# Sliding-window queries computed between the steps of the latent attention, four modulation vectors made by TensorE

## The chip, the cores and the metric

The kernel runs on one core of one Trainium2 chip. The metric is the device time of one execution in microseconds (us). A core has five engines that each take their instructions in order: PE (TensorE, matrix products; its weight loads are listed as PEld), DVE (VectorE), ACT (ScalarE), POOL (GpSimd) and SP (SyncE, which here only issues DMAs; ACT and SP have DMA queues of their own).

## The reference, cut to what matters

The network has 512 tokens of width 1024 and four layers; the change is in the first, the even block: latent attention (MLA, 8 heads) beside sliding-window attention with sinks (SWA, 8 heads, 2 key heads, window 128).

```python
z = h @ w_in
z_cq, z_ckv, z_kr, z_sq, z_sk, z_sv, z_gate = split_cols(z, EVEN_SPLITS)
q  = (rmsnorm(z_cq, q_norm) @ w_uq)      # latent queries, 8 x 96
kv = (rmsnorm(z_ckv, kv_norm) @ w_ukv)   # latent keys and values, 8 x 128
...
o_mla = mla_attention(q_nope, q_rope, k_nope, k_rope, v_mla)
q_s = apply_rope(z_sq, cos_h, sin_h)     # 8 x 64
k_s = apply_rope(z_sk, cos_h, sin_h)     # 2 x 64
o_swa = swa_sink_attention(q_s, k_s, v_s, sinks)
o = jnp.concatenate([o_mla, o_swa], axis=-1) * jax.nn.silu(z_gate)
return o @ w_out
```

Each layer is modulated by vectors of the condition alone: `mod = cond @ ada_w[i] + ada_b[i]` gives scale, shift and gate, each a 1024 x 1024 matrix times a vector. They don't depend on the tokens and are made while other work runs.

## The kernel before

Products of float32 numbers are made as three products of split parts (high x high, high x low, low x high), in the helper `mm3` (L208), so most PE rows of the profile carry L208. Weights are loaded by SP as `raw`, cast by ACT (L222) and their low part made by DVE or POOL (L225). A product of a block of 128 tokens with 512 columns and depth 1024 is 8 x 3 = 24 matmuls of 128x512.

The even block goes through these steps: the input products cq and ckv; SQ (`ev_sq`, 4 blocks of tokens, 96 matmuls of 128x512, rotation on DVE, result written to the DRAM tensor `sq_e`); the latent up-products uq and ukv, written to the DRAM tensor `qk_e` (L852) and read back by heads (L863), where `heads_T` (L650) transposes them in the PSUM tag "tq", which has one bank. `mla()` then runs 16 steps (4 pairs of heads x 4 blocks of queries): scores, softmax (DVE L633 mask and minimum, ACT L635 exponential, DVE L636, POOL L640), transposes of the probabilities (`p_T` L663, L665), and products with the values (L682). `swa()` runs 16 steps of the same kind with at most 256 keys. Both are generators. `weave` runs one step of the attention, and then as many units of a second generator, `fill`, as its share allows; a unit is three matmuls of 512 columns. Before, `fill` holds 72 units: gates 1, 2 and 3 (8 units each), sk (16) and the gates 4, 6, 5, 7. 52 of them go beneath `mla()`. Gate 0 is run ahead. `issue_after` and a scheduler that works from a modelled timeline set the final order of each engine's instructions, so units move somewhat from where the code has them.

The modulation vectors are made by `ada`, piece by piece: each piece (`tick`) loads half a megabyte of the matrix (`araw`, L495, two buffers) and does one step. In the even block four vectors are made, each in 2 halves x 4 steps, 32 steps. Before, the step is `step`: two DVE operations on 128x512 (L540 for the first, else L542), and at the end of a half a group of four small products with ones (L548) and one addition (L550). The other form, `step_pe`, used elsewhere in this program (in the conv stage, L522), lets PE multiply: eight matmuls of 32 columns by 128 in a PSUM bank, then one DVE addition of 128x128 (L524); a step's products are issued one step after its load (`ADA_LAG`).

Of the kernel before, what the change touches and what calls it, by code (L numbers as in the profile page):

```python
# [20 lines left out]
KC = D // P  # L21
# [18 lines left out]
STRICT = 0  # L40
FD = 6
ADA_OFF = 0
W_MLA = 52
ONDVE = (0, 1, 2)
W_FOX = 3
MAIN_OFF = 0
# [13 lines left out]
TV = 0  # L60
TVE = 3
# [3 lines left out]
SQF = 0  # L65
G0 = 2
# [46 lines left out]
class K:  # L113
# [647 lines left out]
    def even(self, act, gs):  # L761
        nc, h = self.nc, self.h
        w = h["ev_w_in"][0]
# [41 lines left out]
            nc.scalar.dma_start(out=sqd[tb * P:(tb + 1) * P, 8:10, :], in_=t.rearrange("p (n d) -> p n d", d=64))  # L805
            nc.scalar.copy(out=SV[:, tb], in_=ps[:, 128:256])

        if TV == 1:
            self.tick_every = TVE
        o = self.otile()  # L810
        if SQF:
            self.run(self.gates(act, w, 1440, o, (0, 1)[:G0]))
        else:
            self.gemm_x(act, w, 672, 512, KC, ev_sq)
        if TV == 2:
            self.tick_every = TVE
        cT = [self.b4() for _ in range(5)]
        for c in range(5):
            ps = self.psum("tp")
# [39 lines left out]
        def mla():  # L859
            self.npool = NPL[0]  # L860
            def load(hd):
                t = self.tmp()[:, :768].rearrange("p (tb d) -> p tb d", d=192)
                nc.scalar.dma_start(out=t, in_=qk[:, hd, :].rearrange("(tb p) d -> p tb d", p=P))  # L863
                return (self.heads_T(t, 96, lambda s, tb: s[:, tb, 0:96], msc),
                        self.heads_T(t, 96, lambda s, tb: s[:, tb, 96:192]))
            nxt = [load(0), load(1)]
            for c in range(4):
                qk2 = nxt
                pv = self.psum("pv")
                for qb in range(NTB):  # L870
                    n = (qb + 1) * P
                    ps = []
                    for qT, kT in qk2:
                        sc = self.scores(slice(0, 96), qT, kT, qb, 0, n)
                        ps.append(self.softmax(sc, n, self.cst[:, C_CM + 512 - n:C_CM + 512]))
                    self.pv_pair(pv, [[V[b][:, h_ * 64:h_ * 64 + 64] for b in range(qb + 1)] for h_ in (2 * c, 2 * c + 1)], ps, qb)
                    if qb in (1, 2) and c < 3:
                        nxt = (nxt if qb == 2 else []) + [load(2 * c + 1 + qb)]
                    yield
                self.tick(TM)  # L880
                self.pv_out(o[:, c, :], pv)

        def swa():
            self.npool = NPL[1]
            t = self.tmp()[:, :512].rearrange("p (tb d) -> p tb d", d=P)
            nc.scalar.dma_start(out=t, in_=sqd[:, 8:10, :].rearrange("(tb p) n d -> p tb (n d)", p=P))
            kT = self.heads_T(t, 128, lambda s, tb: s[:, tb])

            def load(i):
                t = self.tmp()[:, :512].rearrange("p (tb r d) -> p tb r d", r=2, d=64)  # L890
                for r in range(2):
                    nc.scalar.dma_start(out=t[:, :, r, :], in_=sqd[:, i + 4 * r, :].rearrange("(tb p) d -> p tb d", p=P))
                return self.heads_T(t, 128, lambda s, tb: s[:, tb].rearrange("p r d -> p (r d)"), -0.125)

            qTs = {0: load(0), 1: load(1)}
            for hd in (0, 4, 2, 6):
                r = hd // 4
                pv = self.psum("pv")
                for qb in range(NTB):
                    k0 = max(0, qb - 1)  # L900
                    nb = qb - k0 + 1
                    n = nb * P
                    ps = []
                    for h_ in (hd, hd + 1):
                        sc = self.scores(slice(64 * r, 64 * r + 64), qTs[h_ % 4], kT, qb, k0 * P, n)
                        ps.append(self.softmax(sc, n, self.cst[:, C_SM + 256 - n:C_SM + 256], sink=self.nsink[:, h_:h_ + 1]))
                    self.pv_pair(pv, [[SV[:, b, r * 64:r * 64 + 64] for b in range(k0, qb + 1)]] * 2, ps, qb)
                    if hd == 4 and qb < 2:
                        qTs[qb + 2] = load(qb + 2)
                    yield  # L910
                self.tick(TSW)
                self.pv_out(o[:, 4 + hd // 2, :], pv)

        def fill():
            if SQF:
                yield from self.gates(act, w, 1440, o, (0, 1)[G0:])
                yield from self.gemm_xs(act, w, 1184, 256, KC, ev_sk)
                yield from self.gates(act, w, 1440, o, (2,))
                yield from self.gemm_xs(act, w, 672, 512, KC, ev_sq)
                yield from self.gates(act, w, 1440, o, (3, 4, 6, 5, 7))  # L920
                return
            yield from self.gates(act, w, 1440, o, (1, 2, 3))
            yield from self.gemm_xs(act, w, 1184, 256, KC, ev_sk)
            yield from self.gates(act, w, 1440, o, (4, 6, 5, 7))

        self.lo_pool = LOP[0]
        if not SQF:
            self.run(self.gates(act, w, 1440, o, (0,)))
        g = fill()
        self.weave(mla(), 16, g, W_MLA + 16 * SQF)  # L930
        self.weave(swa(), 16, g, (96 - 8 * G0 if SQF else 76) - W_MLA)
        return o


# [706 lines left out]
def build(tc, h, upto=99):  # L1641
    nc = tc.nc
    with ExitStack() as es:
        k = K(tc, h, es)
# [9 lines left out]
        with k.scope(t4=5, xn=1, SB=2, wide=8, wsb=2, rep=1, prow=1, col=1):  # L1654
            cc, cc2, act, gs = k.start(x_in, h["c"], h["c_2"], wa[0], ba[0], h["g_pre"][0], h["ev_w_in"][0], 384)
# [5 lines left out]
        def first(i, mixer, act, xsrc, xdst, wout, **bufs):  # L1661
            with tc.tile_pool(name="xp", bufs=1, reuse_waits="tile") as k.xp:
                with k.scope(**bufs):
                    k.tick_every = TO if i else 1000
                    k.ada_pool = AP[i]
                    rows = [k.ada(cc, wa[i], ba[i], 2048, "gatepost", h["g_post"][i])]
                    if i == 0:
                        rows += [k.ada(cc, wa[1], ba[1], 1024, "scale", h["g_pre"][1]),
                                 k.ada(cc, wa[1], ba[1], 0, "shift")]
                    else:  # L1670
                        rows += [k.ada(cc2, wa2[0], ba2[0], 1024, "scale", h["norm1_g_2"][0]),
                                 k.ada(cc2, wa2[0], ba2[0], 0, "shift")]
                        mods[0] = [k.ada(cc2, wa2[0], ba2[0], 2048, "gate")]
                    if G2 == 2 + i:
                        mods["g2"] = k.ada(cc2, wa2[0], ba2[0], 5120, "gate")
                    o = mixer(act)
                    k.flush()
                    k.lo_pool, k.tick_every = 0, 1
                    k.ada_pool = ()
                    if MK & 4:  # L1680
                        k.mark()
                with k.scope(t4=3, rows=3, oT=2, hl2=3):
                    GG, S, B = [k.spread(r) for r in rows]
                    o = k.out_first(o, wout, xsrc, xdst, GG, S, B)
                    if MK & 8:
                        k.mark()
                    return o

        act = first(0, lambda a: k.even(a, gs), act, x_in, out if upto == 1 else x1, h["ev_w_out"][0], t4=4, ru=1, s=6, pt=6, b4=6, V=4, SV=1)
        if upto == 1:  # L1690
            return
        act = first(1, k.odd, act, x1, out if upto == 2 else x2, h["od_w_out"][0], t4=2, ru=1, hn=1, s=6, pt=6, b4=4, Vd=4, V=4, foxA=1, foxB=1, foxBh=2, lp=1)
        if upto == 2:
            return
# [61 lines left out]
        with tc.tile_pool(name="xp", bufs=1, reuse_waits="tile") as k.xp:  # L1756
            act, xr = second(0, act, k.conv, x2, t4=4, u=3, dw=1, dwr=1, w4=1, u4=4, dg=3)
# [27 lines left out]
        with tc.tile_pool(name="xp", bufs=1, reuse_waits="tile") as k.xp:  # L1785
            act, xr = second(1, act, k.hgrn, x4, V=8, X=3, F=1, op=2, hn=1, gt=1, AT=1, Ad=2, T0=1, T1=1, T2=1, T3=1, T4=1, T5=1, T6=1)
# [41 lines left out]
```

## Time and profile before

| | us |
|---|---|
| median of 3 runs (lowest, highest) | 2098.3 (2095.98, 2098.57) |
| the profiled execution | 2094.94 |
| its span from first to last instruction | 2093.2 |
| PE busy | 1956.3 |
| DVE busy | 1345.0 |
| ACT busy | 861.8 |
| POOL busy | 733.1 |

The span is that of the profiled execution, and all rows below are of it. Busy time is the union of an engine's instructions; PE matmuls overlap each other in the records, so what a matmul costs in a dense stretch is read from the distance of two starts. PEclk is the granted clock of TensorE, 1.00 at 2.4 GHz and 0.50 at 1.2 GHz.

### The profile page before, as it was taken

Reading aid. Unit: us, or ns where it says so; the run is one execution under the profiler, and the core shown is the slowest. Engines: PE = TensorE matmul, PEld = TensorE weight load, DVE = VectorE, ACT = ScalarE, POOL = GpSimd, SP = SyncE. Lnnn points to the kernel's source line nnn. Section 1 sums busy time; section 2 is a strip of 40 time slices with the busy share of each in tenths; the row PEclk is TensorE's granted clock in tenths of the full one; section 3 lists DMA queues with packets and bytes.
Section 4 is the critical chain, followed back from the end, with each engine's and each line's share of the span. In section 5 each row is a group of like instructions: output and inputs, shape, how many; then the busy total and the mean of one; then the engine's idle time right before and its main releaser. Section 6 shows DMA issues by size and latency. Waiting matters only on the chain.

```text
span 2093.2 us, 32588 instructions
## 1 busy us (share of the span) xinstructions
PE 1956.3 (93%) x12759; PEld 1585.6 (76%) x12759; DVE 1345.0 (64%) x1979; ACT 861.8 (41%) x1461; POOL 733.1 (35%) x660
## 2 busy tenths in 40 slices
PE   7799999798999999879899999999999998999998
PEld 5688668565667787458788989877877778898896
DVE  5356775535545479547987748667786858485673
ACT  4345553133554432143434435343554534353452
POOL 1233334221233333015232331456675544223232
PEclk9999979997999999899999999999999999999999
DMA  8484655277343436832554225453322322242331
GB/s 311 129 230 136 180 166 161 80 164 145 80 97 104 149 117 187 223 99 71 178 178 153 87 75 182 134 152 103 103 83 82 121 83 80 91 131 71 121 102 60
DMA packets 225745, 272.09 MB, mean 130 GB/s; under 512 B 26682, under 2 KB 145689, under 8 KB 225592
## 3 DMA queue, kind: packets, MB, share of 16 engines
q1 hardware_dynamic: 188982, 232.83, 37.8%
q10 hardware_dynamic: 36610, 37.18, 5.9%
q8 instruction: 101, 1.65, 0.3%
q14 instruction: 52, 0.43, 0.1%
HBM read 253.57 MB, written 16.40 MB: 129 GB/s over the span
## 4 chain that ended last, share of the span: by engine, by line
PE 41%; DVE 12%; issue 4%; DMA 4%; POOL 2%; ACT 1%; ACTq 0%; SPq 0%; POOLq 0%; DVEq 0%
PE mm L208 23%; PE mm L1223 4%; PE sc L208 4%; PE sc L1223 3%; PE tp L1223 3%; DVE acc L542 2%; DVE ol L1343 2%; DVE hl L201 1%; DMA ud<-u 1%; DVE hl L225 1%; DMA raw<-in_ada_w_dram 1%; PE pv L208 1%; DVE X L1585 1%; DMA u<-ud 1%; DMA raw<-in_mlp_w_dram 0%
## 5 line engine op out<-in xcount | busy, mean ns | idle before, releaser
L208 PE MATMUL mm<-hTh,hl 128*128 128x512 f32 (+2 forms) x1200 | 375.3, 389 | 3.0 <-DVE V L201 1.5
L222 ACT CAST hl<-raw 128x1024 fp32r<-128x1024 f32 (+2 forms) x219 | 224.4, 1033 | 245.7 <-PE mm L208 142.8
L208 PE MATMUL mm<-hl,hid 128*128 128x512 f32 x1344 | 316.9, 395 | 4.9 <-DVE hid L201 3.3
L225 DVE TENSOR_TENSOR hl<-raw,hl 128x1024 fp32r<-128x1024 f32 (+2 forms) x190 | 251.0, 1331 | 78.3 <-ACT hl L222 77.8
L208 PEld LDWEIGHTS mm<-hl,hid 128*128 128x128 f32 x1344 | 251.9, 188 | 64.7 <-DVE hid L201 4.3
L208 PEld LDWEIGHTS mm<-hTh,hl 128*128 128x128 f32 (+1 forms) x1200 | 221.6, 191 | 51.6 <-issue 3.8
L208 PE MATMUL mm<-hl,hTh 128*128 128x512 f32 (+3 forms) x752 | 223.6, 375 | 26.5 <-DVE t L621 11.0
L208 PE MATMUL mm<-hTl,hl 128*128 128x512 f32 (+2 forms) x600 | 232.8, 388 | 0.1
L1140 POOL TENSOR_TENSOR xr<-xr,t 128x512 f32<-128x512 f32 x56 | 80.3, 1433 | 305.6 <-DVE t L1137 304.2
L208 PEld LDWEIGHTS mm<-hl,hTh 128*128 128x128 f32 x752 | 141.8, 199 | 52.2 <-ACT t L788 8.7
L542 DVE SCALAR_TENSOR_TENSOR acc<-araw,ccol,acc 128x512 f32<-128x512 f32 x154 | 135.0, 876 | 36.3 <-DMA araw<-in_ada_w_dram 24.3
L640 POOL TENSOR_TENSOR s<-s,sm 128x256 f32<-128x256 f32 (+3 forms) x112 | 82.8, 740 | 193.1 <-DVE sm L636 184.9
L200 ACT CAST hl<-raw 128x1024 fp32r<-128x1024 f32 x84 | 86.8, 1048 | 135.9 <-PE mm L208 111.3
L208 PE MATMUL mm<-hl,hTl 128*128 128x512 f32 (+3 forms) x376 | 139.8, 372 | 0.4 <-DVE hTl L458 0.4
L201 DVE TENSOR_TENSOR hl<-raw,hl 128x1024 fp32r<-128x1024 f32 x84 | 131.3, 1578 | 13.6 <-ACT hl L200 12.9
L208 PEld LDWEIGHTS mm<-hTl,hl 128*128 128x128 f32 (+1 forms) x600 | 114.5, 191 | 23.6 <-issue 2.0
L1203 POOL TENSOR_TENSOR raw<-raw,raw 128x1024 f32<-128x1024 f32 x28 | 76.2, 2722 | 144.4 <-DVE rows L1203 95.1
L225 POOL TENSOR_TENSOR hl<-raw,hl 128x1024 fp32r<-128x1024 f32 x29 | 73.1, 2520 | 120.5 <-ACT hl L222 120.5
L635 ACT ACTIVATE s<-s,sm 128x256 f32<-128x256 f32 (+5 forms) x128 | 69.6, 544 | 95.0 <-DVE sm L633 89.4
L1137 DVE TENSOR_TENSOR t<-mm,rows 128x512 f32<-128x512 f32 x56 | 38.5, 687 | 106.8 <-PE mm L208 103.1
L208 PE MATMUL sc<-b,b 64*128 64x256 f32 (+7 forms) x384 | 94.5, 361 | 10.5 <-DVE sm L633 8.2
L1588 POOL TENSOR_TENSOR X<-X,T 128x512 f32<-128x512 f32 x56 | 74.2, 1330 | 50.5 <-ACT op L1548 32.7
(366 smaller groups left out, 3960.4 us busy)
## 6 DMA issues: line engine op xcount, KB each, us to landing
raw<-in_mlp_w_dram SPq DMA_DIRECT2D x128, 512.0 KB
araw<-in_ada_w_dram SPq DMA_DIRECT2D x72, 512.0 KB
raw<-in_hgrn_w_in_dram SPq DMA_DIRECT2D x40, 512.0 KB
araw<-in_w_ada_dram SPq DMA_DIRECT2D x32, 512.0 KB
raw<-in_od_w_in_dram SPq DMA_DIRECT2D x32, 512.0 KB
raw<-in_ada_w_dram SPq DMA_DIRECT2D x24, 512.0 KB
rows<-row SPq DMA_DIRECT2D x16, 512.0 KB
raw<-in_conv_w_in_dram SPq DMA_DIRECT2D x16, 512.0 KB
```

The source lines that it names most:

```text
L200: nc.scalar.copy(out=hi, in_=src)
L201: nc.vector.tensor_tensor(out=lo, in0=src, in1=hi.bitcast(F32), op=ALU.subtract)
L208: self.nc.tensor.matmul(out, lhsT=lt[a], rhs=rt[b], start=start and n == 0, stop=stop and n == 2)
L222: self.nc.scalar.copy(out=hi, in_=raw[:, :n])
L225: eng.tensor_tensor(out=lo, in0=raw[:, :n], in1=hi.bitcast(F32), op=ALU.subtract)
L542: eng.scalar_tensor_tensor(out=acc, in0=raw[:, k], scalar=c, in1=acc, op0=ALU.mult, op1=ALU.add)
L635: nc.scalar.activation(out=s[:, :m], in_=s[:, :m], func=AF.Exp, scale=-1.0, bias=mn, accum_out=sm)
L640: nc.gpsimd.tensor_tensor(out=p, in0=p, in1=r.to_broadcast([P, n]), op=ALU.mult)
L1140: eng.tensor_tensor(out=xs, in0=xs, in1=t, op=ALU.add)
L1203: eng.tensor_tensor(out=out, in0=x, in1=y, op=f)
L1223: nc.tensor.matmul(ps[:, m * 256:m * 256 + 256], lhsT=ws[n][:, a, k, m * P:m * P + P], rhs=parts[n][b][:, k], start=m + k + t == 0, stop=m ...
L1588: nc.gpsimd.tensor_tensor(out=xk, in0=xk, in1=cap(Tt, 1, [(row - 1, 2), (2, nb), (0, hh)]), op=ALU.mult)
```

## The change

SQ and gate 0 are no longer run ahead of the attention but are part of `fill`, which now holds 112 units in the order gate 0, sk, gates 1 and 2, SQ, gates 3, 4, 6, 5, 7; 80 go beneath `mla()`. Branches of the old code that were not in use (`SQF`, `TV`) are deleted. In the even block the four vectors are made by `step_pe`, with its products in the PSUM tag "tq", the bank that `heads_T` uses.

```diff
@@ module
-W_MLA = 52
+W_MLA = 80
@@ even(), ahead of the attention
         o = self.otile()
-        if SQF:
-            self.run(self.gates(act, w, 1440, o, (0, 1)[:G0]))
-        else:
-            self.gemm_x(act, w, 672, 512, KC, ev_sq)
...
         def fill():
...
-            yield from self.gates(act, w, 1440, o, (1, 2, 3))
+
+            yield from self.gates(act, w, 1440, o, (0,))
             yield from self.gemm_xs(act, w, 1184, 256, KC, ev_sk)
-            yield from self.gates(act, w, 1440, o, (4, 6, 5, 7))
+            yield from self.gates(act, w, 1440, o, (1, 2))
+            yield from self.gemm_xs(act, w, 672, 512, KC, ev_sq)
+            yield from self.gates(act, w, 1440, o, (3, 4, 6, 5, 7))
 
         self.lo_pool = LOP[0]
-        if not SQF:
-            self.run(self.gates(act, w, 1440, o, (0,)))
         g = fill()
-        self.weave(mla(), 16, g, W_MLA + 16 * SQF)
-        self.weave(swa(), 16, g, (96 - 8 * G0 if SQF else 76) - W_MLA)
+        self.weave(mla(), 16, g, W_MLA)
+        self.weave(swa(), 16, g, 112 - W_MLA)
@@ first()
                     k.ada_pool = AP[i]
+                    k.ada_pe, k.ada_ps = i == 0, "tq"
...
                     k.ada_pool = ()
+                    k.ada_pe = False
```

On PE, just ahead of the first score of the latent attention (`sc`, the row of 128x128), the order before has the gate products (`mm` from `hTh`, `hTl`) around the transposes of the first two heads (L650), and a vector's closing group (L548):

```order
405 L548 MATMUL mm_1513<-acc_1208,ones 32x128 x4
406 L208 MATMUL mm_1441<-hTl,hl_1438 128x512
407 L208 MATMUL mm_1441<-hTh,hl_1438 128x512
408 L650 MATMUL tq_1223<-cst,t_212_1213 96x128 x4
409 L208 MATMUL mm_1583<-hTh,hl_1580 128x512
410 L208 MATMUL mm_1583<-hTl,hl_1580 128x512
```

At the same place the changed kernel has sk's products (128x256), and the two transposes stand back to back:

```order
326 L208 MATMUL mm_1309<-hl_1202,hTl 128x256
327 L208 MATMUL mm_1309<-hl_1202,hTh 128x256
328 L650 MATMUL tq_1034<-cst,t_187_1032 96x128 x4
329 L650 MATMUL tq_1042<-cst,t_187_1032 96x128 x4
330 L208 MATMUL sc_1069<-b_191_1047,b_189_1039 128x128
331 L208 MATMUL mm_1399<-hl_1197,hTh 128x256
```

The first score is row 418 of PE before and row 330 afterwards: SQ, the gates 1 and 2 and a part of 3 have moved behind it, and two of sk's four blocks in front of it.

On PE in the last pair of heads of the latent attention (scores `sc`, transposes `tp`, value products `pv`) the order before has gate products as filler between the attention's own:

```order
660 L663 MATMUL tp_2008<-cst,s_1994 128x128 x3
661 L208 MATMUL sc_2161<-b_422_1945,b_420_1937 128x128 x3
662 L682 MATMUL pv_1823<-pt_2006,V_939 64x128
663 L208 MATMUL mm_2333<-hTh,hl_2330 128x512 x2
664 L208 MATMUL mm_2333<-hTl,hl_2330 128x512
665 L208 MATMUL mm_2333<-hTh,hl_2330 128x512 x2
666 L208 MATMUL mm_2333<-hTl,hl_2330 128x512
```

The changed kernel has steps of the vectors there (L522, in the bank `tq`), and no gate products:

```order
677 L650 MATMUL tq_2053<-cst,t_444_2043 96x128 x4
678 L208 MATMUL sc_2203<-b_448_2058,b_446_2050 128x128
679 L208 MATMUL sc_2259<-b_424_1964,b_422_1956 128x256 x3
680 L522 MATMUL tq_2135<-araw_1982,ccol_93 32x128 x8
681 L208 MATMUL sc_2203<-b_448_2058,b_446_2050 128x128 x2
682 L522 MATMUL tq_2167<-araw_2133,ccol_93 32x128 x8
683 L208 MATMUL sc_2271<-b_448_2058,b_446_2050 128x256 x3
684 L208 MATMUL sc_2312<-b_424_1964,b_422_1956 128x384 x3
685 L663 MATMUL tp_2219<-cst,s_2207 128x128
686 L522 MATMUL tq_2179<-araw_2165,ccol_93 32x128 x8
```

Ten such steps stand in rows 680 to 734; the gate products pause from row 674 to 738 and then reach to row 875, where before the last of them stood some 70 rows ahead of the end of SWA.

On DVE in SWA (row L633 is a softmax's first operation) the order before has an accumulation between almost every two softmaxes:

```order
298 L633 ISA s_2467,sm_2468<-sc_2463,cst,nsink 128x128
299 L633 ISA sm_2468 128x1
300 L542 SCALAR_TENSOR_TENSOR acc_2856<-araw_2865,ccol_93,acc_2856 128x512
301 L636 RECIPROCAL sm_2470<-sm_2469 128x1
302 L633 ISA s_2496,sm_2497<-sc_2492,cst,nsink 128x256
303 L633 ISA sm_2497 128x1
304 L542 SCALAR_TENSOR_TENSOR acc_2856<-araw_2865,ccol_93,acc_2856 128x512
```

The changed kernel has one addition for about two softmaxes:

```order
269 L633 ISA s_2587,sm_2588<-sc_2583,cst,nsink 128x256
270 L633 ISA sm_2588 128x1
271 L524 TENSOR_TENSOR arow_2366<-tq_2727,arow_2366 128x128
272 L636 RECIPROCAL sm_2590<-sm_2589 128x1
273 L633 ISA s_2600,sm_2601<-sc_2596,cst,nsink 128x256
274 L633 ISA sm_2601 128x1
```

The accumulations of 128x512 (L542) are gone from DVE's queue in this stretch, and additions of 128x128 (L524) stand in their place.

## Rows read from the trace of the kernel before

**Rows 1.** page: busy time of each engine, and shares of the chain that ended last:
```profile
PE 1956.3 (93%) x12759; PEld 1585.6 (76%) x12759; DVE 1345.0 (64%) x1979; ACT 861.8 (41%) x1461; POOL 733.1 (35%) x660
...
PE 41%; DVE 12%; issue 4%; DMA 4%; POOL 2%; ACT 1%; ACTq 0%; SPq 0%; POOLq 0%; DVEq 0%
```
**Rows 2.** windows: stages of the even block; columns engines, PEclk, DMA, GB/s:
```profile
80.30:151.40 71.10, 71.10 (x349) 60.26 (x348) 32.79 (x54) 28.12 (x53) 20.55 (x21) 1.00 0.70 186
151.40:168.00 16.60, 14.09 (x72) 11.72 (x72) 10.86 (x28) 7.58 (x21) 5.66 (x7) 0.79 0.62 197
168.00:238.30 70.30, 70.30 (x504) 55.66 (x503) 51.93 (x139) 38.53 (x100) 21.65 (x31) 1.00 0.56 162
238.30:275.00 36.70, 35.04 (x220) 23.92 (x223) 26.31 (x81) 19.04 (x61) 17.85 (x40) 1.00 0.45 130
275.00:308.10 33.10, 31.34 (x147) 19.65 (x147) 22.71 (x65) 15.21 (x50) 12.62 (x26) 0.59 0.56 164
```
**Rows 3.** windows: the start of the latent attention and the tail of SWA:
```profile
151.40:156.60 5.20, 2.69 (x19) 1.94 (x18) 4.67 (x8) 1.93 (x5) 2.38 (x2) 1.00 0.72 216
...
156.60:163.40 6.80, 6.80 (x31) 6.16 (x30) 4.89 (x17) 3.70 (x11) 2.21 (x4) 0.50 0.92 304
...
279.50:306.80 27.30, 27.30 (x116) 17.04 (x116) 17.58 (x53) 11.29 (x39) 10.64 (x21) 0.50 0.58 164
```
**Rows 4.** timeline, PE: dense gate products; first score at 151.44 (start, us, instruction):
```profile
151.21 0.39 PE L208 MATMUL mm<-hTh,hl 128*128 128x512 f32 x1
151.44 0.23 PE L208 MATMUL sc<-b,b 96*128 96x128 f32 x1
```
**Rows 5.** timeline, PE, conv stage: steps of L522 between products:
```profile
821.33 0.63 PE L208 MATMUL mm<-hTh,hl 128*128 128x512 f32 x2
...
821.89 0.64 PE L522 MATMUL tp<-araw,ccol 128*32 128x128 f32 x16
...
822.46 0.50 PE L208 MATMUL mm<-hTl,hl 128*128 128x512 f32 x1
```
**Rows 6.** timeline, PE, SWA: one L548 group and what follows:
```profile
258.75 0.43 PE L548 MATMUL mm<-acc,ones 128*32 128x128 f32 x8
...
259.11 0.43 PE L682 MATMUL pv<-pt,SV 128*64 128x128 f32 x2
...
259.47 0.61 PE L208 MATMUL sc<-b,b 64*128 64x256 f32 x3
```
**Rows 7.** timeline: sinks DMA and the ckv stop:
```profile
58.74 0.28 SPq L779 DMA_DIRECT2D sm<-in_ev_sinks_dram  x1
...
75.15 0.29 PEld L208 LDWEIGHTS mm<-hl,hTh 128*128 128x128 f32 x1 [8.72 <-ACT t L788]
```
**Rows 8.** timeline: qk written, read back and transposed:
```profile
131.69 0.52 ACTq L852 DMA_DIRECT2D qk_e<-t  x1
...
136.49 0.39 ACTq L863 DMA_DIRECT2D t<-qk_e  x1
...
145.14 0.60 PE L650 MATMUL tq<-cst,t 128*96 128x128 f32 x4
```
**Rows 9.** groups of instructions by form, 145 to 308.2: the vector accumulation:
```profile
L542 DVE SCALAR_TENSOR_TENSOR acc<-araw,ccol,acc 128x512 f32<-128x512 f32 x56 | 47.4, 847 | 1.6 <-DMA araw<-in_ada_w_dram 1.4
```
**Rows 10.** windows of L542 alone: DVE busy (count), PEclk, DMA, GB/s:
```profile
238.30:275.00 36.70, 12.15 (x14) 1.00 0.45 130
```
**Rows 11.** timeline, tail of SWA: a softmax behind an accumulation:
```profile
278.87 0.61 PE L208 MATMUL sc<-b,b 64*128 64x256 f32 x3 [0.88 <-DVE sm L633]
...
279.33 0.74 DVE L542 SCALAR_TENSOR_TENSOR acc<-araw,ccol,acc 128x512 f32<-128x512 f32 x1
...
280.07 0.46 DVE L633 CUSTOM_DVE_ANT_0 s<-sc,cst,nsink 128x256 f32<-128x256 f32 x1
```
**Rows 12.** timeline, tail of SWA: araw loads and their first use:
```profile
281.53 0.37 SPq L495 DMA_DIRECT2D araw<-in_ada_w_dram  x1
...
285.99 0.75 DVE L542 SCALAR_TENSOR_TENSOR acc<-araw,ccol,acc 128x512 f32<-128x512 f32 x1 [1.16 <-DMA araw<-in_ada_w_dram]
```

More of the change, by code (lines that the diff above doesn't have):

```diff
@@ L806, in ev_sk @@
             nc.scalar.copy(out=SV[:, tb], in_=ps[:, 128:256])
-        if TV == 1:
-            self.tick_every = TVE
         o = self.otile()
-        if SQF:
-            self.run(self.gates(act, w, 1440, o, (0, 1)[:G0]))
-        else:
-            self.gemm_x(act, w, 672, 512, KC, ev_sq)
-        if TV == 2:
-            self.tick_every = TVE
         cT = [self.b4() for _ in range(5)]
@@ L914, in fill @@
         def fill():
[L915 to L921, printed above, removed]
-            yield from self.gates(act, w, 1440, o, (1, 2, 3))
+            yield from self.gates(act, w, 1440, o, (0,))
             yield from self.gemm_xs(act, w, 1184, 256, KC, ev_sk)
-            yield from self.gates(act, w, 1440, o, (4, 6, 5, 7))
+            yield from self.gates(act, w, 1440, o, (1, 2))
+            yield from self.gemm_xs(act, w, 672, 512, KC, ev_sq)
+            yield from self.gates(act, w, 1440, o, (3, 4, 6, 5, 7))
         self.lo_pool = LOP[0]
-        if not SQF:
-            self.run(self.gates(act, w, 1440, o, (0,)))
         g = fill()
-        self.weave(mla(), 16, g, W_MLA + 16 * SQF)
-        self.weave(swa(), 16, g, (96 - 8 * G0 if SQF else 76) - W_MLA)
+        self.weave(mla(), 16, g, W_MLA)
+        self.weave(swa(), 16, g, 112 - W_MLA)
         return o
```

## The prediction

> **What bounds it now.** I first read the busy times and the chain that ended last [rows 1]: PE (TensorE) is busy 93% of the span and carries 41% of that chain, DVE (VectorE) 12%. So a microsecond of PE work added where PE never waits costs a microsecond, and DVE work counts only where PE waits for it. The second view, busy time by stage [rows 2], shows where PE has room in the stretch that is edited. From 80.3 to 151.4 (last quarter of the ckv product, SQ, uq, ukv, gates) PE is busy throughout. From 151.4 to 168 it is busy 14.1 of 16.6 us at a mean clock of 0.79, from 168 to 238.3 throughout at full clock, and in SWA 35.0 of 36.7 us and then 31.3 of 33.1 us at a mean clock of 0.59. The third view [rows 3] puts the clock in place: 0.50 from 156.6 to 163.4, right behind a stretch in which PE was busy only 2.69 of 5.20 us, and 0.50 from 279.5 to 306.8, where the fillers have run out and PE has the short products of SWA alone.
>
> A busy PE row is not PE at its peak, so I price the work. Two 512-column products in a row start 0.23 us apart [rows 4]. A 256-column one I take at half, 0.12, a 128-column transpose or score at 0.11 and a pv product at 0.2 (two records, with the change of operand, occupy 0.36 [rows 6]; estimates). Latent attention and SWA together then hold 108 gate products (25 us), 96 of sk (11.4), 192 score products (26.5), 136 transposes and 136 pv products (43.4), 76 transposes of heads (8.3) and 8 L548 groups (3.5): 118 us of work in 156.7 us elapsed (151.4 to 308.1). 38.7 us are lost: some 11 in the latent attention, some 27 in SWA. The whole question is how much of the 38.7 the change recovers, since it also adds work.
>
> **The change, term by term.**
>
> *Ahead of the first score.* SQ leaves: 96 products of 0.232 us, 22.3 us. Of gates 0 to 3, 84 products stand there now and 24 afterwards: 60 x 0.232 = 13.9 us less. Two blocks of sk come in, 48 x 0.119 = 5.7 us. Together -30.5 us, and the same work comes back later, so this alone is a wash.
>
> New there is a possible stall. The latent queries and keys go through DRAM: the last write is issued at 131.69, the read back at 136.49, the first transpose starts at 145.14 [rows 8], 13.5 us after the write. The read stood behind a gate's activation in ACT's queue, so some of that is slack; the data path alone I take as 9 to 13 us. Behind the last ukv product there will be 7.8 us of PE work (the rest of gate 0, sk). PE waits between 1 and 5 us; I take 2.5.
>
> The stop at 66 to 75 us stays: ckv's second half waits 8.72 us for ACT, behind POOL's broadcast of the sinks, whose DMA is issued at 58.74 [rows 7]. In the changed order no vector load with a wait stands ahead of that DMA on SP's queue; I take -2.1 us, between 0 and -5.
>
> *The vectors.* Off DVE go 56 L542 operations of 847 ns, 47.4 us in all [rows 9], and 8 L540; 32 additions of 128x128 come instead. Off PE go 8 L548 groups: 0.36 us from a group's start to the next product [rows 6] and 0.08 in front of it, 3.5 us. Onto PE come 32 steps of eight narrow products. This kernel's conv stage has the same step: 0.57 us from its start to the next product, and the two products ahead of it take 0.56 us instead of 0.46 [rows 5], so 0.67 us, 21.4 us for 32 (two steps in a row come a little cheaper; the lower bound is 32 x 0.5 = 16). Net +17.9 us of PE work, all of it in latent attention and SWA, where PE is the bound.
>
> *What is recovered there.* The work in latent attention and SWA becomes 118 + 30.5 + 17.9 = 166.4 us. I sort the lost time by cause.
> The start: 2.5 us idle and 3.4 us of half clock (half of 6.8) [rows 3]. The first softmaxes have nothing ahead of them in either order, so 5.9 stays.
> The rest of latent attention: about 5.5 us over 14 steps, 0.4 a step, while there are 52 units of filler. There will be 80, and no accumulations on DVE, but SQ's rotations instead: 0.3 a step, 4.8.
> SWA: with fillers the first 36.7 us hold 27.3 us of priced work in 8.4 steps: 1.1 us lost a step. L542 takes 12.15 of DVE's 26.31 us there [rows 10, 2], and it stands in the softmax's way: scores that end at about 279.5 are masked only from 280.07, behind an accumulation started at 279.33 [rows 11]. I halve the loss, since one such operation of 0.75 to 0.85 us goes from almost each of the two softmaxes of a step, but only half of them meet it on PE's path: 0.55 x 16 = 8.8 us. Fillers now last to the end (32 units and about 13 vector steps instead of 24 units), so the half clock of the tail goes with its 13.7 us.
> Lost time afterwards: 5.9 + 4.8 + 8.8 = 19.5 us. Elapsed 166.4 + 19.5 = 185.9 against 156.7: +29.2 us.
>
> The half clock tail bears on a rule of the Trainium skill, "TensorE: Matmul & The Clock Gate", section "What's actually happening": the slow clock is the default and activity releases it. The trace agrees: 0.50 in the thin stretch, 1.00 as soon as dense products return [rows 2, 3]. By that rule alone the 13.7 us of the tail come back whole; the sum above has the same.
>
> *Sum.* -2.1 - 30.5 + 2.5 + 29.2 = -0.9 us. The profiled execution took 2094.94 us (span 2093.2), 3.4 us under the median of 2098.3 us of the runs shown; put on the median, 2097 us. The measurement tells changes from 0.2%, 4.2 us, on.
>
> **The rivals.**
>
> *A. Larger gain.* DVE's relief and the filler cover nearly all waits: 2 us in the rest of latent attention, 3 in SWA instead of 13.6, and no wait for qk: -0.9 - 8.6 - 2.5 = -12 us, 2086. For it: PE waits visibly for only few us in SWA with fillers (1.7 of 36.7 [rows 2]). Against: priced work there is three quarters of the time all the same.
>
> *B. Slower: PE waits for the vectors' loads.* PE takes its instructions in order, so an L522 whose half megabyte has not come holds the attention up; DVE so far had room for this wait. A load is issued at 281.53 and first used, after a wait, at 285.99: 4.5 us [rows 12]. Two buffers and a product one step behind its load give at best one step per 2.2 us. In the last pair of the latent attention ten steps stand in 18.4 us of priced PE work, 2.0 us apart, with no other filler between them; and each fills the one "tq" bank that the transposes of heads use too, which must be emptied by DVE first. It decides from the point at which steps come closer than 2.2 us. At 1.3 us each for ten steps and 3 at the rest it costs 16 us; with the same SWA as forecast 2113, and 2105 if half of it is hidden.
> The price of a load by the Trainium skill, "DMA: Bandwidth & Descriptors", section "Anatomy of one DMA — SWDGE (gpsimd) path" (2.0 us and 436 GB/s; another issue path than here), would be 3.2 us, an estimate; the trace says 4.5, and by 3.2 rival B would vanish.
>
> *C. SWA keeps its pace.* Its steps take 4.4 us now with fillers and 4.2 without, at half clock: if the chain score, softmax, transpose sets this and not DVE's load, SWA stays near 1.1 us lost a step, 8.8 us more than forecast, and the time is 2106. For it: the two paces are alike though the clock differs by two. Against: the accumulations lie in that chain in both.
>
> **Numbers.** The forecast, a change of less than a half per cent in which saved and added PE work nearly cancel, has 0.52; its own range is 2088 to 2106 (qk stall, price of a step, sinks), of which 0.20 lies more than 4.2 us under the median, 0.27 within, 0.05 above. A has 0.20, B 0.18, C 0.10. So faster 0.40, same 0.27, slower 0.33. The range leaves out the far half of A and of B: 2084 to 2111.
>
> **What would show it.** First score at about 119 to 122 us instead of 151.4. L522 at 0.5 to 0.7 us a step, no L542 before 310. Latent attention 120 to 130 us long (now 87), SWA 58 to 65 (now 70), its clock near 1.0 throughout. Wrong it would be if PE shows idle time ended by araw DMAs or by DVE L524 of more than 5 us (B), if SWA stays at 69 us or shows half clock (C), or if stages that the diff doesn't touch shift by more than 3 us because the order around them changed.

## The result: 1.3% slower, and the profile after

The changed kernel takes 2128.0 us (median of 4 executions), against 2097.1 us for the kernel before; the ratio is 1.0126, interval 1.0099 to 1.0152. Its profiled execution took 2121.76 us with a span of 2119.7 us, 26.5 us more than the span before. One of the four took 3737.7 us and is left out of the ratio, as one such execution each of `araw_4` and `sq_only_96` is further down. The forecast was 2097 us with a range up to 2111. All times of stages below are read from profiled executions.

The head of the page of the changed kernel, to compare with [rows 1] (busy time of each engine, and the shares of the chain of work that ended last, by engine):

```profile
PE 1973.2 (93%) x13207; PEld 1594.0 (75%) x13207; DVE 1305.0 (62%) x1938; ACT 862.1 (41%) x1461; POOL 727.6 (34%) x661
...
PE 41%; DVE 11%; issue 4%; DMA 3%; POOL 2%; ACT 2%; ACTq 0%; SPq 0%; POOLq 0%; DVEq 0%
```

PE is 17 us busier and DVE 40 us less: the work did move as the diff says, and the chain is still PE's. The next rows are the stages of the changed even block (the four pairs of heads of the latent attention, then SWA), to be held against [rows 2]:

```profile
124.20:156.20 32.00, 30.11 (x162) 25.44 (x163) 13.02 (x39) 13.62 (x34) 10.52 (x13) 0.87 0.38 101
156.20:191.40 35.20, 34.81 (x294) 25.59 (x293) 14.58 (x42) 13.32 (x32) 7.97 (x11) 1.00 0.44 128
191.40:231.10 39.70, 37.28 (x239) 28.06 (x237) 17.99 (x43) 16.92 (x36) 13.03 (x12) 0.96 0.52 163
231.10:262.90 31.80, 23.59 (x268) 15.91 (x266) 12.70 (x42) 10.80 (x29) 6.70 (x14) 0.99 0.63 186
262.90:339.40 76.50, 73.90 (x545) 48.22 (x545) 34.20 (x127) 34.51 (x107) 22.76 (x58) 0.91 0.40 122
```

The first score starts at 124.2 us (151.4 before [rows 4]), so the stretch ahead of it became 27.2 us shorter; 30.1 were forecast. Then the latent attention takes 138.7 us, from 124.2 to 262.9, where it took 86.9, and SWA 76.5 where it took 69.8. The two together take 215.2 us against 156.7. The last pair of heads (231.1 to 262.9) is the odd row: 31.8 us in which PE is busy only 23.59, at nearly full clock. Before, that pair took 19.8 us.

Where the 26.5 us arise: the even block's attention ends 31.3 us later (339.4 against 308.1). From the start to the end of the odd block's attention (its first score of 384 columns to its last L696) the changed kernel is 10.0 us *faster* (511.0 to 712.8, against 480.1 to 691.9), and in what follows 5.6 us slower, for which no run here shows a cause. The odd block is not in the diff; the experiments come back to it.

What the last pair lacks is seen in the products of tile `mm`, nearly all of them fillers (PE busy and count first; the stretches of the third and the fourth pair). The changed kernel:

```profile
191.40:231.10 39.70, 23.64 (x89) 17.35 (x88) 3.78 (x6) 1.20 (x2) 0.96 0.52 163
231.10:262.90 31.80, 2.28 (x8) 1.43 (x8) 0.17 (x1) 0.00 (x0) 0.99 0.63 186
```

88 fillers beneath the third pair (one of the 89 rows had begun before 191.40), 8 beneath the fourth. And this is what PE does with the one "tq" bank at the end of that pair (start, duration, instruction, in brackets what it waited for; a step's eight products are 16 rows):

```profile
249.16 0.64 PE L522 MATMUL tq<-araw,ccol 128*32 128x128 f32 x16
...
250.54 0.64 PE L522 MATMUL tq<-araw,ccol 128*32 128x128 f32 x16
...
253.70 0.64 PE L522 MATMUL tq<-araw,ccol 128*32 128x128 f32 x16 [0.91 <-DMA araw<-in_w_ada_dram]
...
255.79 0.64 PE L522 MATMUL tq<-araw,ccol 128*32 128x128 f32 x16 [0.50 <-DMA araw<-in_w_ada_dram]
...
258.47 0.64 PE L522 MATMUL tq<-araw,ccol 128*32 128x128 f32 x16 [1.02 <-DMA araw<-in_w_ada_dram]
...
259.18 0.29 DVE L524 TENSOR_TENSOR arow<-tq,arow 128x128 f32<-128x128 f32 x1 [0.99 <-PE tq L522]
...
259.52 0.66 PE L650 MATMUL tq<-cst,t 128*128 128x128 f32 x4 [0.40 <-DVE arow L524]
...
260.83 0.69 DVE L201 TENSOR_TENSOR b<-tq,b 128x512 fp32r<-128x512 f32 x1 [1.37 <-ACT b L200]
...
261.58 0.66 PE L650 MATMUL tq<-cst,t 128*128 128x128 f32 x4 [1.40 <-DVE b L201]
...
262.92 0.69 PE L208 MATMUL sc<-b,b 64*128 64x128 f32 x2 [0.69 <-ACT b L203]
```

L522 are steps of the vectors, L650 the transposes of SWA's keys and first queries. Eight steps stand between 239.4 and 258.5 ahead of the first L650, which starts as soon as DVE (L524) has emptied the bank, and the second L650 waits for DVE again. SWA's first score follows at 262.92. The keys that the first of them transposes had been asked for 49 us earlier (kind of instruction, count, duration, first and last start):

```profile
L878 ACTq DMA_DIRECT2D t<-sq_e x1: 425/425/425, 210.9 to 210.9; - x1
```

### The profile page after: what moved, and what is told of

It is laid out like the page before. It is cut to its first block, busy times and chain, and to the rows that moved or that the text cites. A ratio compares the mean times of both kernels' runs of the same rounds, so it can differ in the third digit from the quotient of the medians.

```text
span 2119.7 us, 33452 instructions
## 1 busy us (share of the span) xinstructions
PE 1973.2 (93%) x13207; PEld 1594.0 (75%) x13207; DVE 1305.0 (62%) x1938; ACT 862.1 (41%) x1461; POOL 727.6 (34%) x661
## 4 chain that ended last, share of the span: by engine, by line
PE 41%; DVE 11%; issue 4%; DMA 3%; POOL 2%; ACT 2%; ACTq 0%; SPq 0%; POOLq 0%; DVEq 0%
PE mm L208 22%; PE mm L1209 5%; PE sc L208 4%; PE sc L1209 3%; PE tp L1209 3%; DVE acc L542 2%; DVE ol L1329 2%; PE pv L208 1%; DMA raw<-in_ada_w_dram 1%; DVE hl L201 1%; DVE hl L225 1%; DMA u<-ud 1%; DVE X L1571 1%; DMA ud<-u 1%; PE sc L1348 1%
## 5 line engine op out<-in xcount | busy, mean ns | idle before, releaser
L225 DVE TENSOR_TENSOR hl<-raw,hl 128x1024 fp32r<-128x1024 f32 (+3 forms) x189 | 250.0, 1331 | 85.9 <-ACT hl L222 85.6
L640 POOL TENSOR_TENSOR s<-s,sm 128x256 f32<-128x256 f32 (+3 forms) x112 | 78.1, 698 | 209.3 <-DVE sm L636 196.8
L200 ACT CAST hl<-raw 128x1024 fp32r<-128x1024 f32 x84 | 86.9, 1048 | 136.2 <-PE mm L208 111.3
L542 DVE SCALAR_TENSOR_TENSOR acc<-araw,ccol,acc 128x512 f32<-128x512 f32 x98 | 88.2, 900 | 26.5 <-DMA araw<-in_ada_w_dram 14.0
```

Of the source, the lines that this page charges most:

```text
L200: nc.scalar.copy(out=hi, in_=src)
L225: eng.tensor_tensor(out=lo, in0=raw[:, :n], in1=hi.bitcast(F32), op=ALU.subtract)
L542: eng.scalar_tensor_tensor(out=acc, in0=raw[:, k], scalar=c, in1=acc, op0=ALU.mult, op1=ALU.add)
L640: nc.gpsimd.tensor_tensor(out=p, in0=p, in1=r.to_broadcast([P, n]), op=ALU.mult)
```

## The experiments

Theory Q, formed on these rows: the one bank is handed out in the order of the code. Head transposes and vector steps stand in one line, so a pair's heads are made only when the steps in front of them are through. By this theory the order that the scheduler makes has heads that come at the last moment, fillers drawn forward into the time before, and none left for the last pair. Its rivals are that the move of SQ costs (S), that a step's wait for its load costs (L, which is rival B of the prediction), and that the steps on PE cost by themselves (V). Since nearly every edit changes what the scheduler makes of the whole program, the even block's end (first product of the output projection) is given beside the time. Each ratio is to executions of the kernel before on the same chip. Not every kernel has all 32 steps of the vectors ahead of that end, so the table counts them (16 rows of L522 each), and gives what one costs: the end less that of no_vec_after, which has none, by the count (`-` where there is nothing to compare).

| kernel | first score | first SWA score | end of the even attention | steps ahead of it | us a step | odd attention | time, ratio to before (interval) |
|---|---|---|---|---|---|---|---|
| before | 151.4 | 238.3 | 308.1 | 0 | - | 211.8 | 1 |
| changed | 124.2 | 262.9 | 339.4 | 32 | 1.25 | 201.8 | 1.0126 (1.0099, 1.0152) |
| sq_only | 127.9 | 240.5 | 308.9 | 0 | - | 201.1 | 0.9959 (0.9942, 0.9975) |
| vec_only | 150.5 | 270.5 | 341.3 | 32 | - | 200.3 | 1.0145 (1.0130, 1.0161) |
| no_vec_after | 125.4 | 232.3 | 299.4 | 0 | - | 211.6 | 0.9950 (0.9933, 0.9967) |
| vec_tp | 123.8 | 238.6 | 319.3 | 30 | 0.66 | 201.5 | 1.0055 (1.0037, 1.0072) |
| heads_tp | 121.2 | 251.5 | 327.3 | 32 | 0.87 | 211.5 | 1.0093 (1.0059, 1.0126) |
| one_load | 124.0 | 255.1 | 331.2 | 32 | 0.99 | 201.9 | 1.0080 (1.0049, 1.0111) |
| araw_4 | 126.5 | 266.8 | 344.6 | 32 | 1.41 | 196.0 | 1.0045 (1.0027, 1.0064) |
| sq_only_96 | 128.1 | 241.0 | 306.5 | 0 | - | 209.5 | 0.9980 (0.9962, 0.9999) |
| vec_mm | 122.9 | 239.0 | 317.1 | 32 | 0.55 | 201.0 | 1.0016 (0.9997, 1.0035) |
| vec_swa | 123.7 | 229.8 | 312.8 | 22 | 0.61 | 201.8 | 0.9999 (0.9979, 1.0018) |
| vec_tp_twice | 123.7 | 243.6 | 335.0 | 30, doubled | 1.19 | 206.9 | 1.0083 (1.0053, 1.0112) |

**sq_only**: the changed kernel without its line on the vectors.

```diff
-                    k.ada_pe, k.ada_ps = i == 0, "tq"
```

> Only the move of SQ and gate 0 into the filler (112 units, 80 beneath the latent attention); the four vectors stay on DVE. Theory V (the vectors on PE are what costs): the losses of the attention stay as they were, the time is within about 6 us of the kernel before (2091 to 2103 us). Theory S (the move of SQ is what costs, since it takes the cover from the start of the latent attention and does not bring the softmax chain forward): latent attention and SWA together still lose 48 us or so, the time is 10 us or more above the kernel before.

2090.7 us, ratio 0.9959. S falls: the move of SQ costs nothing in the even block, which ends 0.8 us later than before. It gains nothing there either (see the odd block below for the 9 us).

**vec_only**: the kernel before with that line alone (and the flag reset after the block).

```diff
+                    k.ada_pe, k.ada_ps = i == 0, "tq"
```

> Only the four vectors on PE in the bank of the head transposes; SQ and the gates stand as before. Theory V: 21 us of steps, less 3.5 us of closing groups, plus the waits for loads and for the one bank: 20 to 30 us above the kernel before. Theory S: the vectors fit in SWA's tail, where fillers have run out, and the time is within 8 us of the kernel before.

2130.3 us: the even block ends 33.2 us later, against 31.3 with the whole change. The loss is the vectors', and they lose it with SQ in either place.

**no_vec_after**: the changed kernel, four vectors left out (they are their biases alone).

```diff
+                if self.ada_none:
+                    if q_ == 3:
+                        finish(h_, bias(h_))
+                    return
                 (step_pe if self.ada_pe else step)(h_, q_)
```

> The changed kernel with the four vectors of the even block left out (neither loads nor products; they are their biases alone). It shows what the vectors cost in all. Theory V: from the changed kernel's roughly 2125 us it falls by 25 us or more, to 2100 or lower, and latent attention and SWA lose as little as before. Theory S: it falls by the 21 us of their products at most, and the losses of the two attentions stay near 48 us less the 6 us of waits for loads.

The even block ends at 299.4: the vectors cost 9.5 us there on DVE (308.9 in sq_only) and 40.0 on PE in the changed kernel. It also tells what freeing DVE is worth. Its SWA (busy PE, PEld, DVE, ACT, POOL, then PEclk) first, that of sq_only second:

```profile
232.30:299.40 67.10, 65.45 (x378) 43.68 (x378) 29.58 (x115) 37.03 (x114) 26.63 (x67) 0.95 0.15 48
```

```profile
240.50:308.90 68.40, 65.71 (x394) 43.76 (x393) 46.96 (x141) 34.85 (x109) 31.89 (x62) 0.95 0.49 159
```

DVE is busy 29.58 us instead of 46.96, and SWA, with the same 60 filler products, is 1.3 us shorter; the three closing groups of L548 that PE no longer has there are 1.3 us by the prediction's price. The accumulations did lie in the softmax's way, as in [rows 11], but next to nothing hung on it. Both have a clock of 0.95 there, where SWA before had 1.00 and then 0.59 [rows 2], and yet sq_only's SWA is only 1.4 us shorter than before (68.4 against 69.8): the returned clock was spent on the fillers that came with it, 60 products of 512 columns in place of 33.

**vec_tp**: the changed kernel, vectors in the two banks of the probabilities' transposes.

```diff
-                    k.ada_pe, k.ada_ps = i == 0, "tq"
+                    k.ada_pe, k.ada_ps = i == 0, "tp"
```

> The changed kernel with the vectors' products in the two banks of the probabilities' transposes in place of the one bank of the head transposes. If the one bank holds up the heads (theory B of the prediction, its bank part): 4 to 8 us below the changed kernel. If the bank is no matter, within 3 us of it, apart from what the scheduler orders differently.

2111.5 us; the even block ends at 319.3, 20.1 us earlier than with the heads' bank and 19.9 later than without vectors. So of the 40 us about half is the price of the steps on PE and about half the bank, far more than the 4 to 8 us expected. (Two of the 32 steps come behind that end here, some 1.3 us.) The last two pairs of its latent attention, tile `mm` alone, to be held against 89 and 8 above:

```profile
183.90:215.00 31.10, 14.70 (x57) 10.44 (x57) 3.85 (x6) 0.00 (x0) 1.00 0.56 166
215.00:238.60 23.60, 12.03 (x46) 8.14 (x46) 1.37 (x2) 1.19 (x2) 1.00 0.62 196
```

The fillers are back beneath the last pair, which now takes 23.6 us. All instructions of that pair, and of SWA behind it:

```profile
215.00:238.60 23.60, 23.60 (x196) 18.47 (x194) 12.15 (x37) 12.11 (x29) 4.81 (x8) 1.00 0.62 196
238.60:319.30 80.70, 76.99 (x630) 51.21 (x624) 31.59 (x127) 36.58 (x113) 25.68 (x66) 0.94 0.40 123
```

PE is busy throughout the pair. The same transpose of SWA's keys, and the issue of its load:

```profile
218.09 0.60 PE L650 MATMUL tq<-cst,t 128*128 128x128 f32 x4
```

```profile
L878 ACTq DMA_DIRECT2D t<-sq_e x1: 377/377/377, 210.5 to 210.5; - x1
```

Loaded at the same time as in the changed kernel (210.5 against 210.9), transposed 41 us earlier.

The heads of the latent attention show the same. The last transposes for the third and the fourth pair, in the changed kernel and then in vec_tp:

```profile
193.53 0.61 PE L650 MATMUL tq<-cst,t 128*96 128x128 f32 x4 [1.32 <-DVE sm L636]
...
237.38 0.64 PE L650 MATMUL tq<-cst,t 128*96 128x128 f32 x4
```

```profile
178.96 0.60 PE L650 MATMUL tq<-cst,t 128*96 128x128 f32 x4
...
205.48 0.60 PE L650 MATMUL tq<-cst,t 128*96 128x128 f32 x4
```

In the changed kernel they come 2 and 6 us behind the first score of their pair (191.4 and 231.1), in vec_tp 5 and 9.5 us ahead of it (183.9 and 215.0). Between 156.5 and 185.3 the changed kernel transposes no head at all, while six steps go through the bank (161.7 to 183.0). That is the line of theory Q. The clock is no rival for the 20 us: its mean over both attentions is 0.94 in the changed kernel, 0.95 in vec_tp.

**heads_tp**: the other way round, head transposes in the probabilities' banks, vectors alone in "tq".

```diff
-        ps = self.psum("tq")
+        ps = self.psum(self.heads_tag)
...
+                    k.heads_tag = ("tp", "tq")[i]
```

> The changed kernel with the head transposes of the even block in the two banks of the probabilities' transposes; the vectors keep the one bank for themselves. Theory Q: the bank is handed out in the order of the code, so head transposes stand in line behind vector steps and their loads; apart from the vectors they are free, the even block ends near 319 us as it does with the vectors in the other banks, and the time is 2108 to 2116 us. Theory L (a vector step's wait for its load holds PE up, whatever bank it has): the even block ends at 330 us or later and the time stays above 2120 us.

The even block ends at 327.3, 12 us earlier than changed, and 8 later than Q expected: between the two. Separating heads and vectors helps, but heads then share a line with the probabilities' transposes, which theory Q had left out; SWA's keys are transposed at 248.3, again just ahead of its first score at 251.5. That this second line is what costs the 8 us was not tried. Six of the 32 steps also moved ahead of the first score. The time (2119 us) is no guide, since this kernel has the slower odd block.

**one_load**: three of four loads of the vectors' matrices left out.

```diff
+            if self.ada_ps == "tq" and gk:
+                raw = self.ada_one
+            else:
+                raw = load(half, gk)
+                self.ada_one = raw
```

> The changed kernel with three of four loads of the vectors' matrices left out in the even block (the first piece of each half is used four times, so the vectors come out otherwise); products and bank as changed. Theory Q in its form with loads: the line in the bank moves as fast as DVE empties it, most of the 20 us come back, the even block ends at 322 us or earlier. If the bank alone counts (each step must wait for DVE to empty it), the loads change little: 332 us or later.

331.2, where the bank alone was to give 332 or later and the line with its loads 322 or earlier: between the two. The loads are thus 8 of the 20 us, and the larger part stays without them. The heads stand in the same late places (none is transposed between 155.9 and 184.7).

**araw_4**: four load buffers instead of two (in all places that share the tag).

```diff
-        self.ada_tag, self.ada_raw = "mm", ("araw", 2)
+        self.ada_tag, self.ada_raw = "mm", ("araw", 4)
```

> The changed kernel with four buffers for the loads instead of two, all else equal. By the prediction's rival B the steps' pace is one per 2.2 us because of two buffers; with four it is one per 1.1 us, and the idle time that PE spends for those loads (about 5 us) and what the line in the bank costs fall: the even block ends at 330 us or earlier. If the loads are no limit: within 3 us of 339.

344.6: later, not earlier, so the expectation was missed. Ahead of the steps of the even block (stretch 160 to 345) the changed kernel has this wait among others (us, times), and with four buffers no such row is left:

```profile
  DMA araw<-in_w_ada_dram: 4.5, 5
```

The loads' waits are gone, and hardly any for the bank have come in their place (for DVE's L524 0.5 us instead of 0.2); yet the last pair of the latent attention did not get shorter. All its instructions, 34.7 us against 31.8:

```profile
232.10:266.80 34.70, 32.15 (x267) 20.64 (x266) 12.39 (x42) 10.82 (x29) 6.78 (x14) 0.70 0.57 166
```

PE is idle for 2.6 us instead of 8.2, at a mean clock of 0.70 where the changed kernel had 0.99. The stretch at half clock within the pair:

```profile
239.70:260.20 20.50, 20.50 (x150) 12.62 (x150) 6.88 (x29) 6.20 (x19) 4.97 (x10) 0.50 0.56 153
```

PE is busy all through it, so the clock alone can have cost up to half of its 20.5 us, more than the 5 us by which the end came later. What the buffers are worth at an equal clock therefore stays open: this run neither shows nor rules out that the loads' waits set the pair's length. That the whole kernel is faster than the changed one comes from the odd block (196.0 us), which has an order of its own here.

**sq_only_96**: sq_only with 96 units beneath the latent attention.

```diff
-W_MLA = 80
+W_MLA = 96
```

> Only the move of SQ, vectors on DVE, with 96 instead of 80 units beneath the latent attention. If SWA's length is set by its chain of softmaxes and not by fillers, more work beneath the latent attention lengthens that one to one and shortens SWA little: the even block ends 3 to 8 us later than with 80 (308.9). If fillers matter in neither, the same within 2 us.

306.5, 2.4 us *earlier*: missed in the other direction. The latent attention is 0.3 us longer (112.9 against 112.6) and SWA 2.9 shorter. Part of the reason stands ahead of both: 72 products of sk precede the first score instead of 48, 2.9 us of work by the prediction's price, and yet that score starts only 0.2 us later. So the run does not tell whether fillers beneath SWA are free.

**vec_mm**: vectors in the two banks of the filler products.

```diff
-                    k.ada_pe, k.ada_ps = i == 0, "tq"
+                    k.ada_pe, k.ada_ps = i == 0, "mm"
```

> The changed kernel with the vectors' products in the two banks of the filler products. Theory Q (the line in the one bank of the head transposes costs 20 us, whatever else): heads are free of the vectors, pairs of heads overlap again, the even block ends at 316 to 324 us, as with the probabilities' banks (319.3). Theory P (it was these other banks that suit the vectors, for instance by their order): the even block ends above 330 us.

317.1, as Q said. It is not the probabilities' banks that suit the vectors; it is the heads' bank that does not.

**vec_swa**: the one "tq" bank as changed, but no steps beneath the latent attention.

```diff
-        self.tick_every = 1
+        self.tick_every = 1000
...
-                self.tick(TM)
...
+                    self.tick(2)
                     yield
...
-                self.tick(TSW)
```

> The changed kernel, vectors in the one bank of the head transposes as changed, but no vector step beneath the latent attention: two for each step of SWA. Theory Q: in SWA only two head transposes are left behind vector steps, so the latent attention is as short as without vectors (near 107 us, first SWA score at 231 to 236 us instead of 263), and the even block ends at 315 to 325. If it is not the line but the number of vector products or their loads, what the latent attention gains comes back in SWA and the block ends near 339.

The same bank and the same loads and buffers, with the steps elsewhere. Its latent attention and its SWA, all instructions, and then the steps (L522) in SWA alone:

```profile
123.70:229.80 106.10, 104.33 (x611) 82.70 (x612) 50.41 (x139) 50.95 (x124) 35.02 (x40) 0.96 0.31 91
229.80:312.80 83.00, 79.75 (x729) 52.47 (x729) 36.42 (x140) 36.87 (x114) 26.60 (x67) 0.96 0.53 159
```

```profile
229.80:312.80 83.00, 16.82 (x352) 9.23 (x352) 0.96 0.53 159
```

The latent attention takes 106.1 us, as without vectors (106.9), and the even block ends at 312.8, 26.6 us earlier than changed and just ahead of the 315 to 325 expected. But 352 rows are 22 steps: the other ten come behind that end, from 319.8 to 374.8. The stretch from the even block's end to the odd block's first score is 172.2 us instead of the 164.2 of the changed kernel, so of the 26.6 us 18.6 are left by then. For the 22 steps in SWA the price is 0.61 us each, as in vec_tp and vec_mm, in the very bank in which they cost 1.25 with the heads behind them.

**vec_tp_twice**: vec_tp with each step's products made twice.

```diff
-                for k in range(2):
+                for _ in range(2 if self.ada_twice else 1):
+                    for k in range(2):
```

> The kernel with the vectors in the probabilities' banks, with the eight products of each of the 32 steps made twice. The price of a step on PE, 0.67 us, is 0.57 at least for the products alone: the even block ends 16 to 21 us later than 319.3 if PE is the bound there, less than 8 us later if the steps lie in gaps of the softmax chain.

15.7 us more in the even block, just under what was expected. As in vec_tp, 30 of the steps come ahead of its end: 0.52 us for each doubling, near the 0.57 of a step's products. PE is the bound there, and the steps find hardly any gaps.

**The odd block.** Its attention took 200 to 202 us in seven kernels, 207 to 212 in five, and 196 in araw_4. Read from the built programs, PE's instructions there stand in exactly the same order in before, no_vec_after, heads_tp, sq_only_96 and vec_tp_twice (the five), and in exactly one other order in the changed kernel, sq_only, vec_only, vec_tp, one_load, vec_mm and vec_swa (the seven). Before and no_vec_after, which have the first order:

```profile
480.10:691.90 211.80, 200.56 (x985) 142.25 (x985) 111.50 (x295) 99.32 (x221) 61.76 (x60) 0.92 0.45 105
```

```profile
475.50:687.10 211.60, 199.77 (x985) 141.83 (x985) 111.36 (x295) 99.46 (x221) 62.36 (x60) 0.92 0.43 104
```

sq_only and the changed kernel, which have the second:

```profile
481.50:682.60 201.10, 192.78 (x985) 136.76 (x985) 110.50 (x295) 98.90 (x221) 61.51 (x60) 0.95 0.47 110
```

```profile
511.00:712.80 201.80, 193.72 (x986) 137.55 (x986) 110.46 (x295) 98.96 (x221) 61.49 (x60) 0.95 0.49 110
```

The count of PE's instructions is the same within one, the time differs by 10 us, the mean clock is 0.92 against 0.95. The order goes with the time and not with what was edited in the even block. A part of the 10 us is the clock's: vec_tp_twice has the first order at a mean clock of 0.95, and its 206.9 us are 5 more than the second order takes at that clock, 5 fewer than the first at 0.92. Why the scheduler came to the one or the other was not tried.

## Why the prediction was wrong

The forecast was a near cancellation, -0.9 us. By its own terms:

*Ahead of the first score* (-30.1 forecast with the sinks' 2.1, -27.2 measured). The moved work was right. The two head transposes back to back in one bank and the data path through DRAM cost 3.1 us of waits on PE in place of 2.5:

```profile
120.46 0.64 PE L650 MATMUL tq<-cst,t 128*96 128x128 f32 x4 [0.99 <-DMA t<-qk_e]
...
122.50 1.07 PE L650 MATMUL tq<-cst,t 128*96 128x128 f32 x4 [1.41 <-DVE b L204]
...
124.24 0.47 PE L208 MATMUL sc<-b,b 96*128 96x128 f32 x1 [0.67 <-ACT b L200]
```

The ckv stop gave back 1.0 us and not 2.1: the second half starts at 74.14, where it started at 75.15 [rows 7], behind a wait as long as before:

```profile
74.14 0.29 PEld L208 LDWEIGHTS mm<-hl,hTh 128*128 128x128 f32 x1 [8.88 <-ACT t L788]
```

The remaining 1.2 us are not accounted for.

*Work added by the vectors on PE* (+17.9 net). In size this held: 0.57 us from a step to the next product in the changed kernel too, 21.0 us in the 32. In the two free banks 30 steps cost 19.9 us against no vectors, 0.66 each where 0.67 was forecast. Against the vectors on DVE that is 10.4 us (319.3 against 308.9), since DVE's version was not free either: it cost 9.5.

*What is recovered there* is the step that failed. The prediction had 19.5 us lost in the two attentions after the change (elapsed time less the work at its prices); by the same prices they lost 215.2 - 166.4 = 48.8. Two causes.

The first, 18 to 20 us, is the bank. With the steps out of the heads' way the loss is 30.4 us in vec_tp, 28.4 in vec_mm and 29.4 in vec_swa (each by its own count of steps in the stretch), as without any vectors (29.0). The prediction listed the bank in rival B as a detail beside the loads and gave the rival 0.18; it sized B by the loads, at 2.2 us a step from two buffers. By the Trainium skill's price of a load ("DMA: Bandwidth & Descriptors", "Anatomy of one DMA — SWDGE (gpsimd) path"), which the prediction set beside its own, B would have vanished. The trace does not agree: PE waited 4.5 us in five places for these loads. Shown is this: without three quarters of the loads 8 us come back (one_load), with steps and heads in different banks 12, 20 or 22 (heads_tp, vec_tp, vec_mm), and with the steps moved out of the heads' way in the same bank 19 (vec_swa, up to the odd block's first score). The prediction had read off the order that ten steps stood in the last pair with no filler between (in the trace the tenth comes behind SWA's first score), and took it for a place where the loads might be late; by these runs it was the visible end of a line that began at the heads. How much of the 20 us is waiting on the bank at run time and how much is the order that was built around it was not separated; PE's idle time in the last pair is 8.2 us, a part of it for loads, so most of the 20 should be order. One_load, whose heads come as late with most of the loads gone, points the same way, but no run separates the two.

The second, about 10 us, is DVE's relief and the tail. Lost time was to fall from 38.7 us by half of SWA's and the whole tail. In sq_only, with fillers to nearly the end, 181.0 us elapsed for 148.5 us of work by the same prices: 32.5 us lost. Without vectors at all, DVE 17 us freer in SWA, 29.0 (174.0 elapsed, 145.0 of work). In vec_tp, with 30 steps in the stretch, it is 195.5 - 165.1 = 30.4. So SWA's pace was not set by the accumulations (rival C was right in that), and the halved loss a step was wishful: one row of a softmax behind an accumulation [rows 11] shows that a delay occurs, not that the chain hangs on it.

The clock's return in the tail, 13.7 us by the prediction, did come in sq_only (27.3 us at half clock before, 6.8 there), but it was spent: SWA got 1.4 us shorter with 27 more filler products in it, which are 6.3 us at the prediction's price. In the changed kernel SWA's mean clock was 0.91, where near 1.0 was forecast. One reading behind that term was loose: in [rows 3] the clock is still 1.00 in the thin stretch and 0.50 behind it, with PE busy 6.80 of 6.80 us, so that it returns as soon as dense products do is more than those rows show. Two slips in the price of the work are too small to matter: transposes of probabilities stand in the sum at 0.119 us and not at the 0.11 named (1.2 us), and one of the eight L548 groups lies ahead of the first score (0.4 us).

That the kernel lost 26.5 us and not 31.3 comes from the odd block, 10.0 us faster in its other order, which no term of the prediction had (it had only named such shifts as a thing to look for), less the 5.6 us behind it that stay open.

**A version that beats both**: sq_only, 2090.7 us, 0.9959 (0.9942, 0.9975). Its gain arises in the odd block, which the edit does not touch; the even block is level.

## What to carry to other kernels

A tile tag with one buffer acted here as a queue in the order of the code: before putting a second user into one, list who stands behind whom, and ask what the last in line feeds. With steps in front of the heads' transposes a step cost 1.25 us on the mean, in the same bank with all of them beneath SWA 0.61, half of it. Count, too, what has moved out of a stretch before calling the stretch faster: ten of vec_swa's steps had. And an edit in one block can come with another order in a block that it does not touch: compare stage by stage, and do not credit an edit with a gain that arises where it did nothing.

## What the runs showed that I had not expected

With four load buffers PE's idle time in the last pair fell from 8.2 to 2.6 us, and the granted clock went to 0.50 for 20.5 us in the same stretch, so that the pair took 2.9 us more. Two orders of the same instructions in the odd block differ by 10 us in 212 (5%), with the mean granted clock at 0.92 in the slower and 0.95 in the faster, and by 5 us where both have 0.95.
